# Four modulation chunks computed beside attention on VectorE instead of beside the deltanet on TensorE

## The chip, the cores and the metric

The kernel runs on one core of a Trainium2 chip. The metric is the device time of one execution in microseconds (us). The engines are TensorE (PE: matmuls, and PEld: its weight loads), VectorE (DVE), ScalarE (ACT), GpSimd (POOL) and SyncE (SP, which here issues nearly all DMA transfers). Each takes its instructions in the order in which the program holds them and waits at the first that isn't ready.

## What is computed

The reference is two blocks of a network over 512 tokens of width 1024. The first has a recurrence (hgrn2), a gated deltanet and a mixture of experts (MoE). The second has two layers: attention with a convolutional feed-forward part, then a gated unit with another. Each layer of the second block shifts, scales and gates its activations with a modulation vector, made from one conditioning vector:

```python
m_lat = (s_c @ ada_w[l] + ada_b[l])[:, None, :]          # 1024 -> 6 * 1024
sh1, sc1, g1, sh2, sc2, g2 = jnp.split(m_lat, N_MOD, axis=-1)
h_lat = modulate_2(rms_norm_2(x, mix_norm[l]), sh1, sc1)
...
x = x + g1 * y_lat
x = x + g2 * conv_ffn(modulate_2(rms_norm_2(x, ffn_norm[l]), sh2, sc2), ...)
```

The change is on this product for l = 0. The kernel cuts its 6144 columns into twelve chunks of 512, each with 2 MB of weights. Chunks 0 to 5 give sh1, sc1 and g1; chunks 6 to 9 give sh2 and sc2, which are first read by the normalisation ahead of the feed-forward part, behind attention; 10 and 11 give g2.

## The kernel before

All weights are float32 and come from memory once, each when it is used. A large product splits both sides into a high and a low part (whi and wlo from wraw or wrawx, hhi and hlo from the activations, lines 267 to 273) and adds three matmuls (lines 530 to 532). ScalarE makes the high parts and mostly VectorE the low ones.

The program is written as stages, and inside a stage as generators that are stepped in turn: in_turn (line 128) keeps up to `most` parts active, steps each once a turn, and steps `fill` once a turn too; what is left of fill when the parts are done runs behind them. Where an instruction stands on its engine is decided after that: the tile framework schedules the whole program with a simulated timeline, so work can be placed ahead of its place in the text where its data allow it. The order that results is fixed when the kernel is built.

There are two ways to make a modulation chunk:

- matvec_steps (line 334) on TensorE: two loads of 1 MB (wraw), eight matmuls of 512 columns whose stationary side is the conditioning vector (line 355), a copy on ScalarE (sq, line 359), four transposes (line 363), and two short sums on VectorE (mred, mod).
- matvec_on_dve (line 371) on VectorE: four loads of 512 KB (mvr), eight products of 128 x 512 with a per-partition scalar, added up in one tile (mva, lines 383 and 385), four transposes on TensorE (line 388), a reduction (mred, line 390) and a short sum into mod (line 391). The pool has one buffer of mva, and `bufs` of mvr.

```python
acc = pool.tile([P, 512], F32, name="mva")
...
nc.vector.tensor_scalar(acc, raw[:, k, :], c, None, op0=ALU.mult)
...
nc.vector.scalar_tensor_tensor(acc, raw[:, k, :], c, acc, op0=ALU.mult, op1=ALU.add)
```

The stages that the change touches, in order of time:

- The deltanet's core (dn_core, line 1199): twelve chunks of tokens, five active at a time, a new one every third turn. Its steps are small matmuls with copies and masked copies between them on ScalarE and VectorE. Its fill is matvec_steps with nine chunks of the modulation, one at two turns.
- The end of the MoE and the normalisation ahead of attention: TensorE makes the attention's projections of the context (hc in the tile hthi, pool hh) while moe_add adds the experts' result to x; then rstds_of_two (line 450) makes two inverse roots, one after the other, each with a step on GpSimd (rr, lines 456 to 463), TensorE spreads them, and norm_mod (lines 479 to 482) writes hhi and hlo for the projections of the latent tokens.
- The attention's core (attention_core, line 1676): eight heads in the order 0, 1, 4, 5, 6, 7, 2, 3, each with four units of 128 queries, three units active. A unit has scores (sc, line 1598), a maximum on VectorE (smax, line 1605), an exponential on ScalarE, transposes (line 1616; pT, line 1617) and the product with the values (av, lines 1742 and 1751). Heads 4 to 7 are differential: GpSimd adds two score tiles (line 1736), and VectorE normalises the result (qa, line 1789). The next head's operands are stacked in between (st, ks, kg, lines 1577 and 1588).
- The output projection (to_feature, line 637, and out_proj, line 554): TensorE transposes four blocks (line 650), which are split into hhi and hlo; the weights' splits whi and wlo are made beside them.

Of the kernel before, what the change touches and what calls it, by code (L numbers as in the profile page):

```python
# [127 lines left out]
def in_turn(parts, most, every, fill=None, newest=False):  # L128


    parts, active, turn, more = iter(parts), [], 0, True
    while active or more:
        if more and len(active) < most and turn % every == 0 or not active:
            part = next(parts, None)
            more = part is not None
            if more:
                active.append(part)
        turn += 1
        for part in list(active[::-1] if newest else active):
            if next(part, active) is active:  # L140
                active.remove(part)
        next(fill or iter(()), None)
    for _ in fill or ():
        pass
# [81 lines left out]
class Kern:  # L226
# [141 lines left out]
                                 bias[:, ch * 4:ch * 4 + 4].unsqueeze(2).to_broadcast([P, 4, 2]))  # L368
            yield

    def matvec_on_dve(self, pool, cc, w, bias, out, chunks, nk=2, bufs=3):

        nc = self.nc
        for ch in chunks:
            acc = pool.tile([P, 512], F32, name="mva")
            for k0 in range(0, KD, nk):
                raw = pool.tile([P, nk, 512], F32, name="mvr", bufs=bufs)
                nc.sync.dma_start(raw.rearrange("p k c -> p (k c)"), w.at(k0 // 4 * 4, 4, [(ch * 512, 512)])
                                  [:, k0 % 4 * 512:(k0 % 4 + nk) * 512])
                for k in range(nk):  # L380
                    c = cc[:, k0 + k, 0:1]
                    if k0 + k == 0:
                        nc.vector.tensor_scalar(acc, raw[:, k, :], c, None, op0=ALU.mult)
                    else:
                        nc.vector.scalar_tensor_tensor(acc, raw[:, k, :], c, acc, op0=ALU.mult, op1=ALU.add)  # L385
            p = self.ps.tile([P, 4, P], F32, name="aux", tag="aux")
            for s in range(4):
                nc.tensor.transpose(p[:, s, :], acc[:, s * P:s * P + P], self.ident)  # L388
            red = self.sp.tile([P, 4, 2], F32, name="mred")[:, :, 0]
            nc.vector.tensor_reduce(red, p, axis=AX.X, op=ALU.add)  # L390
            nc.vector.tensor_add(out[:, ch * 4:ch * 4 + 4, 0], red, bias[:, ch * 4:ch * 4 + 4])
            yield
# [1280 lines left out]
            wide(1024, [t["va"][:, a:b]])  # L1673
        return t

    def attention_core(self, t):

        nc = self.nc
        cp = self.pool("acore", 1)
# [73 lines left out]
            if qt == 3:  # L1753
                self.gqa_out(cp, t["qb"][:, :, i * P:i * P + P], av, sm)

        in_turn((unit(n, qt) for n in range(8) for qt in range(4)), 3, 1, None, True)

    def gqa_out(self, pool, o, av, sm):

# [155 lines left out]
def build(tc, aps):  # L1915
    nc = tc.nc
    with ExitStack() as ctx:
        K = Kern(ctx, tc, aps)
# [4 lines left out]
        cc = K.silu_cols("c", "c_ctx")  # L1923
        cc2 = K.silu_cols("c_2", "c_ctx_2")
        mod, mod0, mod1 = (K.cp.tile([P, 48, 2], F32, name=f"mod{n}") for n in range(3))
        ada0 = lambda f, chunks, *a: f(cc2, K.weights("ada_w_2"), K.vec("ada_b_2", 0, 48), mod0, chunks, *a)
        w, w_mod = K.weights("w_in"), K.weights("w_mod")
# [7 lines left out]
        with K.phase():  # L1935
            mp = K.pool("mix")
            oxh = mp.tile([P, 4, 512], F32, name="oxh")
            with ExitStack() as hstack:
                h = K.new_h(hstack.enter_context(tc.tile_pool(name="h", bufs=1, side="right")))
                with K.phase():  # L1940
                    hgp = K.pool("hgp")
                    hs0 = hgp.tile([P, 2, 4, P], F32, name="hs0")
                    t = {"v": hgp.tile([P, 4, 512], F32, name="hgv"), "kq": hgp.tile([P, 4, 3, T], F32, name="hgkq")}
                    with K.phase(4, 3):
                        hc = K.new_h(K.pool("hpc"), TC)
                        K.side = "right"
                        with K.phase():
                            xp = K.pool("xp")
                            with K.phase():
                                wm = K.matvec_steps(cc, w_mod, K.vec("b_mod"), mod, range(4), K.pool("mv"), 4)  # L1950
                                next(wm)
                                xc, accc = K.load_x(xp, aps["ctx"], TC, "xcT")
# [9 lines left out]
                        with K.phase():  # L1962
# [4 lines left out]
                            with tc.issue_after(K.loaded.ins):  # L1967
                                next(first)
                                x, acc = K.load_x(K.sp, aps["x"], T, t["kq"].rearrange("p h c t -> p (h c) t")[:, 0:KD, :])
# [38 lines left out]
                    xc, x, ab = K.dn_proj(st, h, w, oxd, dnd)  # L2008
                    K.split_on = [(None, None)]
            with K.phase(5, 0):  # L2010
                K.dn_core(op, xc, x, ab, ds0, oxd, ada0(K.matvec_steps, (0, 1, 2, 3, 4, 6, 7, 8, 9)))
            dstack.close()
            xp = ctx.enter_context(tc.tile_pool(name="xp", bufs=1, side="right"))
            x = K.reload(xp.tile([P, KD, T], F32, name="xT"), aps["x"])
# [23 lines left out]
        with K.phase():  # L2038
            K.wlp = K.pool("wl", 4)
            with K.phase(5, 0, 4):  # L2040
                K.moe(sd, reload_hc, ysd, hd, x, bs, mod, lambda pool: ada0(K.matvec_steps, range(5, 6), pool, 2, True))
            qp, st = right(qstack, "qst"), right(astack, "astore")
            with K.phase(4, 0, 1):
                hl = K.pool("hp")
                K.side = "right"
                with K.phase():
                    fn = K.vec("final_norm_w")
                    sums = K.pool("sums", space=PSUM).tile([P, 4, 2], F32, name="sums")
                    with K.phase():
                        K.moe_add(K.pool("ysp"), sums, ysd, x, mod[:, 40:48, :], fn)  # L2050
                    K.side = None
                    bx, bs = K.rstds_of_two(sums)
                    wn = K.sp.tile([P, KD], F32, name="wn")
                    nc.vector.tensor_mul(wn, mn, fn)
                    h = K.norm_mod(K.new_h(hl), x, bs, wn, mod0, 0, 1, 0)
                    K.scale_by(x, bx, fn)
                t = K.attention_proj(st, qp, (hc, h))
        with K.phase():
            K.attention_core(t)
        astack.close()  # L2060
        hstack.close()
        with K.phase(4):
            hp = K.pool("hp")
            with K.phase():
# [49 lines left out]
```

## Time and profile before

| | us |
|---|---|
| median of 3 runs (2381.67 to 2384.58) | 2383.46 |
| profiled execution: its own time | 2387.35 |
| profiled execution: span, first to last instruction | 2385.5 |
| TensorE matmuls busy | 2240.5 (94%) |
| VectorE busy | 1614.3 (68%) |
| ScalarE busy | 1200.8 (50%) |
| GpSimd busy | 620.3 (26%) |

Busy shares are averages over the span. A view by windows gives the same for a stretch; a timeline gives single instructions with their start, their duration and, in brackets, the idle time ahead of them with what ended it. Instructions of one kind that overlap are merged into one row (x8 is eight records). The granted clock is a share of TensorE's 2.4 GHz. All times are from the start of the span.

### The profile page before, as it was taken

The page shows a single profiled execution, that of the slowest core. Times are in us where ns is not written, and L with a number is a line of the kernel's source. Part 1 is how long each engine was busy: PE and PEld are TensorE (multiplying, and loading weights), DVE is VectorE, ACT ScalarE, POOL GpSimd, SP SyncE. Part 2 cuts the span into 40 slices and gives each one's busy share as a digit, 9 for nine tenths or more (in the row PEclk, how much of TensorE's full clock was granted, in tenths as well). Part 3 has the DMA queues.
Part 4 walks back from the last instruction along what each step waited for, and adds up shares of the span by engine and source line. Part 5 has one row for each costly group of instructions (what it writes and reads, how often), then busy time and mean ns, then how long its engine had stood idle before and what let it go on. Part 6 is the DMA issues. An engine that isn't in the chain of part 4 may idle for free.

```text
span 2385.5 us, 33834 instructions
## 1 busy us (share of the span) xinstructions
PE 2240.5 (94%) x13058; PEld 1880.5 (79%) x13058; DVE 1614.3 (68%) x2545; ACT 1200.8 (50%) x1969; POOL 620.3 (26%) x470
## 2 busy tenths in 40 slices
PE   6998989989988899999999999999999999999998
PEld 3988977758875677778778878878888988888887
DVE  4777877778855888886857865896673445553553
ACT  4455644456754677776337763432342433432433
POOL 2133544345421111100441422332333001110111
PEclk9999999999999899999999999999999999999999
DMA  8564004151045799997210002656433222323321
GB/s 317 186 222 143 28 1 153 46 219 74 2 177 230 281 395 368 372 379 267 77 39 1 2 36 107 237 193 231 148 131 102 102 89 71 106 73 113 106 74 60
DMA packets 68405, 355.24 MB, mean 149 GB/s; under 512 B 8065, under 2 KB 12817, under 8 KB 37009
## 3 DMA queue, kind: packets, MB, share of 16 engines
q1 hardware_dynamic: 62752, 333.94, 38.0%
q0 software_dynamic: 5488, 19.11, 3.3%
q8 instruction: 104, 1.70, 0.3%
q14 instruction: 61, 0.49, 0.1%
HBM read 334.45 MB, written 19.40 MB: 148 GB/s over the span
## 4 chain that ended last, share of the span: by engine, by line
PE 43%; DVE 5%; issue 1%; ACT 1%; DMA 0%; POOL 0%; SPq 0%; POOLq 0%; DVEq 0%; ACTq 0%
PE mm L531 12%; PE mm L532 12%; PE mm L530 12%; PE sc L1598 2%; PE av L1751 1%; PE aux L1616 1%; DVE mva L385 1%; PE av L1742 1%; DVE smax L1605 1%; DVE wlo L273 1%; PE aux L1587 0%; DVE cy L1868 0%; PE aux L388 0%; DVE st L1577 0%; DVE alo L273 0%
## 5 line engine op out<-in xcount | busy, mean ns | idle before, releaser
L530 PE MATMUL mm<-hhi,whi 128*128 128x512 f32 (+1 forms) x1184 | 438.0, 375 | 10.3 <-ACT whi L270 5.3
L531 PE MATMUL mm<-hlo,whi 128*128 128x512 f32 (+1 forms) x1184 | 441.5, 374 | 2.9 <-DVE hlo L482 2.9
L532 PE MATMUL mm<-hhi,wlo 128*128 128x512 f32 (+1 forms) x1184 | 438.7, 372 | 0.0
L270 ACT CAST whi<-wraw 128x1024 fp32r<-128x1024 f32 (+1 forms) x240 | 246.3, 1041 | 300.1 <-PE mm L531 223.5
L273 DVE TENSOR_TENSOR wlo<-wraw,whi 128x1024 fp32r<-128x1024 f32 (+1 forms) x203 | 249.3, 1244 | 179.9 <-ACT whi L270 179.1
L273 DVE TENSOR_TENSOR wlo<-wrawx,whi 128x1024 fp32r<-128x1024 f32 x190 | 229.0, 1230 | 94.3 <-ACT whi L270 93.0
L270 ACT CAST whi<-wrawx 128x1024 fp32r<-128x1024 f32 (+1 forms) x210 | 215.0, 1048 | 154.2 <-PE mm L531 106.1
L530 PEld LDWEIGHTS mm<-hhi,whi 128*128 128x128 f32 x1184 | 224.8, 191 | 49.4 <-ACT whi L270 5.9
L531 PEld LDWEIGHTS mm<-hlo,whi 128*128 128x128 f32 x1184 | 225.9, 191 | 41.5 <-DVE hlo L482 3.3
L532 PEld LDWEIGHTS mm<-hhi,wlo 128*128 128x128 f32 x1184 | 225.4, 191 | 38.0 <-issue 0.2
L530 PE MATMUL mm<-whi,hhi 128*128 128x512 f32 (+1 forms) x640 | 218.2, 346 | 6.3 <-ACT hhi L481 2.3
L532 PE MATMUL mm<-whi,hlo 128*128 128x512 f32 (+1 forms) x640 | 219.9, 347 | 3.8 <-DVE hlo L482 3.7
L531 PE MATMUL mm<-wlo,hhi 128*128 128x512 f32 (+1 forms) x640 | 219.6, 345 | 0.5 <-DVE wlo L273 0.4
L385 DVE SCALAR_TENSOR_TENSOR mva<-mvr,cc_c,mva 128x512 f32<-128x512 f32 x154 | 156.6, 1017 | 3.4 <-DMA mvr<-in_w_mod_dram 1.2
L1878 POOL TENSOR_TENSOR cy<-cy,csg 128x512 f32<-128x512 f32 x44 | 64.7, 1472 | 348.0 <-DVE cy L1870 332.5
L531 PE MATMUL mm<-alo,whi 128*128 128x512 f32 (+1 forms) x396 | 145.0, 366 | 0.0
L530 PE MATMUL mm<-ahi,whi 128*128 128x512 f32 (+1 forms) x396 | 144.7, 367 | 0.0
L532 PE MATMUL mm<-ahi,wlo 128*128 128x512 f32 (+1 forms) x396 | 144.4, 366 | 0.0
L273 POOL TENSOR_TENSOR wlo<-wraw,whi 128x1024 fp32r<-128x1024 f32 (+1 forms) x37 | 90.1, 2434 | 203.7 <-ACT whi L270 195.4
L530 PEld LDWEIGHTS mm<-whi,hhi 128*128 128x128 f32 x640 | 125.1, 196 | 20.3 <-ACT hhi L481 2.8
L532 PEld LDWEIGHTS mm<-whi,hlo 128*128 128x128 f32 x640 | 124.9, 196 | 19.7 <-DVE hlo L482 6.2
L531 PEld LDWEIGHTS mm<-wlo,hhi 128*128 128x128 f32 x640 | 125.0, 196 | 14.4 <-DVE wlo L273 1.3
(548 smaller groups left out, 4672.4 us busy)
## 6 DMA issues: line engine op xcount, KB each, us to landing
wrawx<-in_w_down_dram SPq DMA_DIRECT2D x32, 1024.0 KB, 9.1
wrawx<-in_w_gate_dram SPq DMA_DIRECT2D x30, 1024.0 KB, 9.0
wraw<-in_w_up_dram SPq DMA_DIRECT2D x30, 1024.0 KB, 9.2
wraw<-in_ffn_w_up_dram SPq DMA_DIRECT2D x30, 1024.0 KB, 4.8
mvr<-in_ada_w_dram SPq DMA_DIRECT2D x56, 512.0 KB, 4.5
wraw<-in_ada_w_dram SPq DMA_DIRECT2D x20, 1024.0 KB, 4.9
wraw<-in_w_in_dram SPq DMA_DIRECT2D x18, 1024.0 KB, 6.9
mvr<-in_w_mod_dram SPq DMA_DIRECT2D x32, 512.0 KB, 4.4
```

What stands on the lines that cost most here:

```text
L270: nc.scalar.copy(hi, src)
L273: (lo_eng or nc.vector).tensor_sub(lo, src, hi.bitcast(F32))
L385: nc.vector.scalar_tensor_tensor(acc, raw[:, k, :], c, acc, op0=ALU.mult, op1=ALU.add)
L530: nc.tensor.matmul(out, ahi, bhi, start=start, stop=False)
L531: nc.tensor.matmul(out, ahi, blo, start=False, stop=False)
L532: nc.tensor.matmul(out, alo, bhi, start=False, stop=stop)
L1598: nc.tensor.matmul(s[:, a:a + n], qs[:, qt * P:qt * P + P], ks[i][:, a:a + n], start=i == 0, stop=i == 1)
L1605: nc.vector.tensor_reduce(m, s[:, :768], axis=AX.X, op=ALU.max, negate=True)
L1616: nc.tensor.transpose(tp[:, j, :], p[:, (a + j) * P:(a + j + 1) * P], self.ident)
L1742: nc.tensor.matmul(av[:, qt, :], pt[:, k, :], hd["v"][:, k, :], start=k == 0, stop=k == 5)
L1751: nc.tensor.matmul(av[j * 64:j * 64 + 64, qt, :], hd["v"][:, k, :], pt[:, k, :], start=k == 0, stop=k == 5, tile_position=(0, j * 64))
L1878: nc.gpsimd.tensor_mul(y, y, sg)
```

## The change

Chunks 6 to 9 leave the fill of the deltanet's core, which keeps 0 to 4. The attention's core gets a fill: matvec_on_dve for these four, with three buffers of mvr and a new parameter, apart, that gives up five turns behind each load's two products. The pool for it is opened ahead of the attention's core, and the stack that holds hthi is closed before it, so that the loads' buffers and the accumulator can lie where hthi was.

```diff
-    def matvec_on_dve(self, pool, cc, w, bias, out, chunks, nk=2, bufs=3):
+    def matvec_on_dve(self, pool, cc, w, bias, out, chunks, nk=2, bufs=3, apart=0):
...
                         nc.vector.scalar_tensor_tensor(acc, raw[:, k, :], c, acc, op0=ALU.mult, op1=ALU.add)
+                for _ in range(apart):
+                    yield
...
-    def attention_core(self, t):
+    def attention_core(self, t, fill):
...
-        in_turn((unit(n, qt) for n in range(8) for qt in range(4)), 3, 1, None, True)
+        in_turn((unit(n, qt) for n in range(8) for qt in range(4)), 3, 1, fill, True)
...
-                K.dn_core(op, xc, x, ab, ds0, oxd, ada0(K.matvec_steps, (0, 1, 2, 3, 4, 6, 7, 8, 9)))
+                K.dn_core(op, xc, x, ab, ds0, oxd, ada0(K.matvec_steps, range(5)))
...
+        hstack.close()
         with K.phase():
-            K.attention_core(t)
+            mv = K.pool("mv")
+            K.attention_core(t, K.matvec_on_dve(mv, cc2, K.weights("ada_w_2"), K.vec("ada_b_2", 0, 48), mod0, range(6, 10), 2, 3, 5))
         astack.close()
-        hstack.close()
```

In the changed program most lines carry a number that is higher by one to three, so line 385 is 386 there. Three places of the order show where the scheduler put the work. The first is VectorE between the MoE and the attention; before:

```order
L536 SCALAR_TENSOR_TENSOR xT<-aux,mod_79,xT 128x512 x4
L273 TENSOR_TENSOR wlo<-wraw,whi 128x1024
L456 TENSOR_SCALAR rr_11553<-sums 128x8
L457 TENSOR_SCALAR rr_11553<-rr_11553 128x4
L459 TENSOR_TENSOR rr_11553<-rr_11553 128x4
L460 TENSOR_TENSOR rr_11553<-rr_11553 128x4
L461 TENSOR_SCALAR rr_11553<-rr_11553 128x4
L463 TENSOR_TENSOR rr_11553<-rr_11553 128x4
L479 SCALAR_TENSOR_TENSOR nmt<-xT,nma,aux 128x256 x4
```

and with the change:

```order
L273 TENSOR_TENSOR wlo<-wraw,whi 128x1024
L384 TENSOR_SCALAR mva<-mvr,cc_c_75 128x512
L386 SCALAR_TENSOR_TENSOR mva<-mvr,cc_c_75,mva 128x512 x2
L459 TENSOR_SCALAR rr_11461<-sums 128x8
L386 SCALAR_TENSOR_TENSOR mva<-mvr,cc_c_75,mva 128x512
L460 TENSOR_SCALAR rr_11461<-rr_11461 128x4
L386 SCALAR_TENSOR_TENSOR mva<-mvr,cc_c_75,mva 128x512 x2
L462 TENSOR_TENSOR rr_11461<-rr_11461 128x4
...
L466 TENSOR_TENSOR rr_11461<-rr_11461 128x4
L386 SCALAR_TENSOR_TENSOR mva<-mvr,cc_c_75,mva 128x512
L482 SCALAR_TENSOR_TENSOR nmt<-xT,nma,aux 128x256 x4
L386 SCALAR_TENSOR_TENSOR mva<-mvr,cc_c_75,mva 128x512
```

All eight products of chunk 6 now stand among the two inverse roots. On SyncE, three of its loads stand behind the weight load ahead of them, then one more weight load, then the fourth.

The second is VectorE at the end of the attention's core; qb is the last head's output, the splits under it belong to the output projection; before:

```order
L1617 COPY pT<-aux 128x384 x3
L1768 TENSOR_TENSOR qb<-qb,av 128x4x128
L273 TENSOR_TENSOR wlo<-wraw,whi 128x1024
L273 TENSOR_TENSOR hlo_14802<-aux,hhi_14801 128x512
L273 TENSOR_TENSOR wlo<-wraw,whi 128x1024
L273 TENSOR_TENSOR hlo_14802<-aux,hhi_14801 128x512 x3
L273 TENSOR_TENSOR wlo<-wrawx,whi 128x1024 x2
```

and with the change:

```order
L1620 COPY pT<-aux 128x384 x4
L393 TENSOR_REDUCE mred<-aux 128x4
L384 TENSOR_SCALAR mva<-mvr,cc_c_75 128x512
L1771 TENSOR_TENSOR qb<-qb,av 128x4x128
L394 TENSOR_TENSOR mod_80<-mred,vec 128x4
L386 SCALAR_TENSOR_TENSOR mva<-mvr,cc_c_75,mva 128x512 x7
L393 TENSOR_REDUCE mred<-aux 128x4
L394 TENSOR_TENSOR mod_80<-mred,vec 128x4
L475 SCALAR_TENSOR_TENSOR nma<-mod_80,vec 128x8
L273 TENSOR_TENSOR wlo<-wraw,whi 128x1024 x2
L273 TENSOR_TENSOR wlo<-wrawx,whi 128x1024 x2
L273 TENSOR_TENSOR hlo_14814<-aux,hhi_14813 128x512 x4
```

Seven products and the reduction of chunk 9 stand between qb and the splits, and all four wlo now come ahead of the first hlo. On SyncE, eight loads of mvr (the eighth to fifteenth) stand behind the attention's small loads, then the wrawx load of the output projection, then the sixteenth load of mvr.

The third is TensorE at the same place; before:

```order
L1751 MATMUL av<-pT,kv 64x128 x6
L650 MATMUL aux<-cst,qa 128x128 x4
L1751 MATMUL av<-pT,kv 64x128 x5
L650 MATMUL aux<-cst,qa 128x128 x8
L530 MATMUL mm<-hhi_14801,whi 128x512 x2
L650 MATMUL aux<-cst,qa 128x128 x4
L531 MATMUL mm<-hlo_14802,whi 128x512
```

and with the change:

```order
L1754 MATMUL av<-pT,kv 64x128 x6
L391 MATMUL aux<-cst,mva 128x128 x4
L1754 MATMUL av<-pT,kv 64x128 x5
L391 MATMUL aux<-cst,mva 128x128 x4
L653 MATMUL aux<-cst,qa 128x128 x12
L533 MATMUL mm<-hhi_14813,whi 128x512 x4
L653 MATMUL aux<-cst,qa 128x128 x4
L534 MATMUL mm<-hlo_14814,whi 128x512
```

The transposes of chunk 8 stand where four of the projection's stood, and those of chunk 9 ahead of all twelve. Chunk 7's eight products stand on VectorE behind the second differential head's sums (odr), one at a time between the maxima and splits of the next heads; those of chunk 8 stand likewise in the last two heads. In the feed-forward stage behind, the same fourteen chunks are made as before, with a few products in other places.

## Rows read from the trace of the kernel before

**Rows 1.** The page, part 1: busy us, share of the span, instructions.

```profile
PE 2240.5 (94%) x13058; PEld 1880.5 (79%) x13058; DVE 1614.3 (68%) x2545; ACT 1200.8 (50%) x1969; POOL 620.3 (26%) x470
```

**Rows 2.** Windows, deltanet's core: us, busy (x instructions) by engine, clock, DMA.

```profile
514.52:562.57 48.05, 44.69 (x482) 35.46 (x480) 36.00 (x63) 31.89 (x64) 19.73 (x18) 1.00 0.51 196
562.57:606.47 43.90, 40.76 (x446) 37.20 (x444) 39.64 (x78) 30.70 (x64) 24.87 (x21) 1.00 0.00 1
```

**Rows 3.** Timeline of TensorE, one chunk in the core: start, us, instruction.

```profile
521.62 1.92 PE L355 MATMUL aux<-wraw,cc_c 128*32 128x512 f32 x16
...
523.48 0.40 PE L1018 MATMUL mm<-dnxi,dny 128*128 128x128 f16 x4
...
527.86 0.61 PE L363 MATMUL aux<-cst,sq 128*128 128x128 f32 x4
...
528.30 0.39 PE L1018 MATMUL mm<-dnxi,dny 128*128 128x128 f16 x4
```

**Rows 4.** Timeline of TensorE: the last matmul that reads the context's activations.

```profile
1131.13 0.40 PE L532 MATMUL mm<-whi,hthi 128*128 128x512 f32 x1
```

**Rows 5.** Tile mvr: ns min/median/max of the products, and the loads' landing.

```profile
L385 DVE SCALAR_TENSOR_TENSOR mva<-mvr,cc_c,mva x154: 734/748/2986, 77.5 to 1772.7; 128x512 f32<-128x512 f32 x154
...
L383 DVE TENSOR_SCALAR mva<-mvr,cc_c x22: 475/479/2491, 77.0 to 1760.7; 128x512 f32<-128x512 f32 x22
...
DMA to landing us min/median/max: 3.2/4.5/7.7
```

**Rows 6.** Timeline of VectorE, chain of the inverse roots.

```profile
1133.13 1.23 DVE L273 TENSOR_TENSOR wlo<-wraw,whi 128x1024 fp32r<-128x1024 f32 x1 [1.50 <-ACT whi L270]
...
1135.72 0.17 DVE L456 TENSOR_SCALAR rr<-sums 128x8 f32<-128x8 f32 x1 [1.37 <-PE sums L1510]
...
1137.25 0.16 DVE L459 TENSOR_TENSOR rr<-rr 128x4 f32<-128x4 f32 x1 [1.16 <-POOL rr L431]
...
1140.42 1.66 DVE L479 SCALAR_TENSOR_TENSOR nmt<-xT,nma,aux 128x256 f32<-128x256 f32 x4 [1.33 <-PE aux L438]
```

**Rows 7.** Windows, attention's core: differential heads, then the last two heads.

```profile
1345.00:1360.00 15.00, 12.56 (x94) 11.30 (x93) 14.98 (x32) 11.86 (x26) 5.42 (x6) 1.00 0.00 1
...
1405.00:1424.00 19.00, 19.00 (x205) 15.14 (x201) 8.64 (x15) 8.94 (x21) 0.00 (x0) 1.00 0.00 1
```

**Rows 8.** Line 390, the reduction of one chunk: ns min/median/max.

```profile
L390 DVE TENSOR_REDUCE mred<-aux x22: 679/688/693, 93.4 to 1782.3; 128x4 f32<-128x512 f32 x22
```

**Rows 9.** Timeline of VectorE: the four qa products of two heads.

```profile
1347.21 2.96 DVE L1789 SCALAR_TENSOR_TENSOR qa<-od,odss,subln 128x128 f32<-128x128 f32 x4
...
1370.65 1.13 DVE L1789 SCALAR_TENSOR_TENSOR qa<-od,odss,subln 128x128 f32<-128x128 f32 x4
```

**Rows 10.** Timeline of GpSimd beside the first of these.

```profile
1347.40 1.86 POOL L1736 TENSOR_TENSOR pexp<-pexp 128x768 f32<-128x768 f32 x1 [1.96 <-ACT pexp L1735]
```

**Rows 11.** Timeline of TensorE behind the last head.

```profile
1423.71 0.87 PE L1751 MATMUL av<-pT,kv 128*64 128x128 f32 x10
...
1428.11 0.48 PE L531 MATMUL mm<-hlo,whi 128*128 128x512 f32 x1
```

**Rows 12.** Timeline of VectorE behind the last head.

```profile
1424.69 0.69 DVE L1768 TENSOR_TENSOR qb<-qb,av 128x512 f32<-128x512 f32 x1 [2.79 <-PE av L1751]
1425.82 1.22 DVE L273 TENSOR_TENSOR wlo<-wraw,whi 128x1024 fp32r<-128x1024 f32 x1 [0.44 <-ACT whi L270]
1426.96 0.68 DVE L273 TENSOR_TENSOR hlo<-aux,hhi 128x512 fp32r<-128x512 f32 x1
```

**Rows 13.** Timeline of SyncE's queue at the same place.

```profile
1424.72 0.33 SPq L506 DMA_DIRECT2D wrawx<-in_attn_w_out_dram  x1
```

**Rows 14.** Windows, behind an idle TensorE: PEclk stands after POOL's time.

```profile
681.00:690.00 9.00, 3.24 (x25) 2.92 (x25) 4.98 (x8) 5.82 (x19) 4.40 (x3) 0.91 0.45 141
690.00:695.00 5.00, 5.00 (x14) 3.87 (x15) 5.00 (x14) 4.18 (x11) 1.02 (x1) 0.50 1.00 382
```

## The prediction

> **What bounds the kernel now.** I read the share of busy time first: TensorE is busy 94% of the span, VectorE 68% [rows 1]. That is an average over unlike stages, so next come the stretches in which the change takes away and adds work, each with its busy times, and then the order of single instructions in them.
>
> Four stretches matter. In the deltanet's core, from 514.5 to 562.6 us, TensorE is busy 44.69 of 48.05 us and VectorE 36.00; in the 43.90 us behind it, where no modulation chunk is left, TensorE has 40.76 and VectorE 39.64 [rows 2]. Each stretch holds three starts of a chunk of tokens. Both engines bound this core. Between the MoE and the attention, VectorE runs a short serial chain (two inverse roots) on which TensorE waits [rows 6]. In the differential heads VectorE is the bound: 14.98 of 15 us, TensorE 12.56 [rows 7]. In the last two heads it is TensorE, 19.00 of 19, and VectorE has 8.64 [rows 7]. Behind the last head VectorE's splits (wlo, hlo) release the first matmuls of the output projection [rows 11, 12].
>
> **What is taken away: the deltanet's core.** Four of nine chunks leave. TensorE's 16 records of one chunk fill it from 521.62 to 523.48, 1.86 us, and its four transposes from 527.86 to 528.30, 0.44 us [rows 3]: 2.30 us a chunk, 9.2 us for four, all inside 514.5 to 562.6. What that is worth has two bounds. If TensorE alone sets the pace, 44.69 - 9.2 = 35.5 us of work at the later stretch's busy share (40.76 / 43.90 = 0.93) take 38.2 us: 9.9 us gained. If these three rounds of the core cannot get shorter than the three behind them (43.90 us), 4.2 us. VectorE lies between: 36.00 us at its share there (39.64 / 43.90 = 0.90) take 39.9 us, 8.1 us gained. I take **-8**, since VectorE is the next bound; the ends are -9.9 and -4.2. The four copies on ScalarE (busy 31.89 of the 48.05 us) and the eight short sums on VectorE that go too, and the eight loads, are counted at nothing: the work beside them goes on as before.
>
> **What is added, in four places.** A chunk is four loads of 512 KB, a first product of 0.48 us and seven of 0.75 us on VectorE [rows 5], four transposes (0.44 us, as above) and a reduction of 0.69 us [rows 8]: 5.7 us of products, 6.4 us in all. The short sum into mod is left out of the count.
>
> *Chunk 6, in the chain of inverse roots.* The order puts three products ahead of the first step (rr from sums), one behind it, two in the first wait for GpSimd, one ahead of the first normalisation (nmt) and one behind it. The buffers lie where the context's activations lay, and the last matmul that reads those begins at 1131.13 and takes 0.40 [rows 4]; so the first load goes out at 1131.5 and lands 3.2 us later at the soonest, 4.5 at the median [rows 5]: 1134.7 to 1136.0. VectorE is free at 1134.4, and rr began at 1135.72 [rows 6]. Three products (0.48 + 2 x 0.75) put it at 1136.7 to 1138.0: 1.0 to 2.3 late. The product behind it adds 0.75; the two inside the wait (1.5 us in about 1.2) add 0.3; the one ahead of nmt needs the fourth load, which reuses the first buffer and goes out behind a weight load, so it lands some 4.5 us after 1136.5, at 1141, when nmt (1140.42 before) has already slid to 1142.5; the last adds 0.75. Sum 2.8 to 4.1; TensorE waits for this chain. I take **+3**; the ends are +1.5 (the products fill idle time of VectorE) and +5 (the fourth load lands after 7.7 us, the maximum of its row).
>
> *Chunk 7, in the differential heads.* Its 6.4 us fall on the stretch in which VectorE is full [rows 7]; about 1 us of idle just ahead takes up some. Then there is GpSimd: the four qa products took 2.96 us where a GpSimd sum of 1.86 us ran beside them, and 1.13 us the second time [rows 9, 10], so an operation of VectorE that meets one waits 1.8 us. I take **+5.5**; the ends are +2 (TensorE has 2.4 us of idle in which to catch up, and later heads have slack) and +8 (two such meetings).
>
> By the Trainium skill, page SBUF — State Buffer, section Who interferes with whom, a VectorE instruction with two inputs in SBUF and a GpSimd one that reads SBUF exclude each other for a whole instruction. These rows agree: 2.96 less 1.13 is the length of the sum beside it. Taken for each of the two or three sums that stand there, the rule would make this term about 9 and the total 17.
>
> *Chunk 8, in the last heads.* TensorE is full, VectorE half idle: the products hide. The transposes of chunks 6 to 8 do not (3 x 0.44). **+1**, ends 0 and +2.5.
>
> *Chunk 9, behind the last head.* This is the largest term. A chunk has one accumulator, and chunk 8's transposes stand five matmuls before the last av on TensorE; chunk 9's first product waits for them. So seven of its products stand on VectorE behind the last qb product, ahead of all splits for the output projection; and on TensorE its transposes stand ahead of all the projection's transposes and matmuls. The time: qb ends at 1425.4 [rows 12]; products two to six, 5 x 0.75, end at 1429.1. The last two need the sixteenth load, whose buffer is free only after the second product (1426.2) and which stands in SyncE's queue behind the 1 MB wrawx load of 1424.72 [rows 13]: with 4.5 us it lands at 1430.7, and the products end at 1432.2. Transposes 0.44, reduction 0.69: 1433.3. Then four wlo, 1.14 us apart (1425.82 to 1426.96, [rows 12]), and the first hlo, 0.6: 1438.5. The first matmul on hlo began at 1428.11 [rows 11]; it slides by 10.4, less 0.5 since two more L530 matmuls now stand ahead of it. TensorE is nearly idle meanwhile; after it had been busy only 3.24 of 9 us elsewhere, the granted clock was 0.50, the 1.2 GHz level, for 5 us [rows 14], in which half of 5 us of work is lost. I take **+12**; the ends are +7.5 (the sixteenth load is there in time, no clock loss) and +15 (it lands after 7.7 us, and the clock falls).
>
> **Sum.** -8 + 3 + 5.5 + 1 + 12 = +13.5 us. The profiled execution took 2387.35, so 2400.9; it stands 3.9 above the median of the runs, 2383.46, so **2397.0** as such a median.
>
> **Rivals.**
> 1. *Faster.* TensorE is at 94% and VectorE at 68%: four chunks leave the full engine and hide on the other. For it: chunk 8's place. Against it: the order at the end, where VectorE is not idle cover but the only way to the projection. If all products hid, -8 and 4 x 0.44 of transposes give -6.2: 2377. It decides at the last av: chunk 9 would have to be reduced by 1428.1, and its first product cannot begin before 1424. Chance 0.07. The Trainium skill, page Perfetto Trace Analysis, section Identifying the Most-Contended Engine, says to optimise the engine of highest occupancy first; going by that alone this would be the outcome, and the rows of this case speak against it.
> 2. *No change to be told.* The core gains all 9.9, the sixteenth load is in time (+7.5), chunks 6 and 7 cost their low ends (3.5): +1 to +4.5, 2385 to 2388. For it: the low ends share one cause, loads that land early. Chance 0.15.
> 3. *Much slower.* The core's rounds keep the later length (-4.2), GpSimd meets the products twice, the sixteenth load is held by wrawx: 5 + 8 + 2.5 + 15 - 4.2 = +26, 2410. Above +20 it has a chance of 0.13.
>
> **The numbers.** A forecast of +5 to +20 keeps 0.65. A measurement of this kernel tells 0.2%, 4.8 us, from no change. Slower by more: 0.65 + 0.13 = 0.78; within: 0.15; faster: 0.07. The range runs from 2386 (+2.5: rival 2's upper part is in) to 2407 (+23.5); the ends of all terms together, +1 and +26, are less likely than 2 in 10.
>
> **What would show it.** Right: the core's stretch with five chunks shortened by 7 to 9 us; eight products among the inverse roots, nmt 2 to 4 us later against the end of the context's matmuls; between the last av and the first hlo matmul some 14 us instead of 3.5, with TensorE waiting on mva and the clock near 0.50 behind it; products on the chain in the differential heads. Wrong: a gap behind the last av under 8 us (then the sum is near zero), a core shortened by less than 4 or more than 10, or a change of several us in the feed-forward stages, whose products only change places and which I count at nothing.

## The result and the profile after

The changed kernel takes 2406.93 us (median of four runs), the kernel before beside it 2382.57: a ratio of 1.0105, 95% interval 1.0087 to 1.0122. It is slower by 21 to 29 us. The forecast was 2397.0; 2406.9 lies at the upper end of the range, and the ratio times the median of 2383.46 gives 2408.5, just above it. The profiled execution took 2406.73, with a span of 2404.9: 19.4 more than the one shown of before, where 13.5 were forecast.

The page of the changed kernel, part 1, answers to [rows 1]: VectorE has 20.8 us more work, and TensorE, from which four chunks were taken, is no less busy.

```profile
PE 2240.0 (93%) x12994; PEld 1882.9 (78%) x12994; DVE 1635.1 (68%) x2577; ACT 1202.4 (50%) x1965; POOL 621.2 (26%) x470
```

The windows of the deltanet's core, columns as in [rows 2]: the same three rounds, then the three behind them.

```profile
512.83:553.27 40.44, 36.04 (x402) 32.16 (x400) 32.14 (x56) 29.58 (x60) 21.09 (x18) 1.00 0.07 26
553.27:597.17 43.90, 40.81 (x445) 37.15 (x443) 38.27 (x77) 30.97 (x64) 25.16 (x21) 1.00 0.01 1
```

48.05 us became 40.44: 7.6 gained. Then VectorE's timeline among the inverse roots; it answers to [rows 6].

```profile
1127.70 0.49 DVE L384 TENSOR_SCALAR mva<-mvr,cc_c 128x512 f32<-128x512 f32 x1 [1.37 <-DMA mvr<-in_ada_w_dram]
1128.22 1.54 DVE L386 SCALAR_TENSOR_TENSOR mva<-mvr,cc_c,mva 128x512 f32<-128x512 f32 x2
1129.68 0.16 DVE L459 TENSOR_SCALAR rr<-sums 128x8 f32<-128x8 f32 x1
...
1134.54 0.75 DVE L386 SCALAR_TENSOR_TENSOR mva<-mvr,cc_c,mva 128x512 f32<-128x512 f32 x1 [0.42 <-DMA mvr<-in_ada_w_dram]
1135.45 1.66 DVE L482 SCALAR_TENSOR_TENSOR nmt<-xT,nma,aux 128x256 f32<-128x256 f32 x4 [0.16 <-PE aux L441]
```

VectorE waits 1.37 us for the first load and 0.42 for the last, and seven of the eight products stand ahead of nmt. Last, the timelines of four engines behind the last head, put together in order of time; [rows 11 to 13] show the place before.

```profile
1425.85 0.87 PE L1754 MATMUL av<-pT,kv 128*64 128x128 f32 x10
1426.87 0.33 SPq L509 DMA_DIRECT2D wrawx<-in_attn_w_out_dram  x1
1426.96 0.68 DVE L1771 TENSOR_TENSOR qb<-qb,av 128x512 f32<-128x512 f32 x1
1427.57 6.28 POOL L273 TENSOR_TENSOR hlo<-qb,hhi 128x512 fp32r<-128x512 f32 x4 [31.68 <-ACT hhi L270]
1427.62 9.13 DVE L386 SCALAR_TENSOR_TENSOR mva<-mvr,cc_c,mva 128x512 f32<-128x512 f32 x7
1429.42 0.33 SPq L379 DMA_DIRECT2D mvr<-in_ada_w_dram  x1
1436.90 1.09 PE L391 MATMUL aux<-cst,mva 128*128 128x128 f32 x4 [10.19 <-DVE mva L386]
1437.78 2.77 PE L653 MATMUL aux<-cst,qa 128*128 128x128 f32 x12
1439.11 2.36 DVE L273 TENSOR_TENSOR wlo<-wraw,whi 128x1024 fp32r<-128x1024 f32 x2
1441.39 2.35 DVE L273 TENSOR_TENSOR wlo<-wrawx,whi 128x1024 fp32r<-128x1024 f32 x2
1443.66 1.88 DVE L273 TENSOR_TENSOR hlo<-aux,hhi 128x512 fp32r<-128x512 f32 x3
1445.12 0.77 PE L534 MATMUL mm<-hlo,whi 128*128 128x512 f32 x1
```

TensorE waits 10.19 us for the products. Its first hlo matmul begins 17.0 us later than before, and the last row of av only 2.1 us later. Behind the wait its granted clock is at the 1.2 GHz level (window, columns as in [rows 14]); and ScalarE, whose casts whi stand ahead of every wlo, had by the profile waited for chunk 9's transposes too (its timeline; before, whi waited 1.56 us for av):

```profile
1436.90:1440.00 3.10, 3.10 (x15) 3.10 (x16) 1.90 (x4) 1.97 (x3) 0.00 (x0) 0.50 0.00 0
1438.03 2.00 ACT L270 CAST whi<-wraw 128x1024 fp32r<-128x1024 f32 x2 [8.97 <-PE aux L391]
```

The seven products take 9.13 us, where seven of 0.75 are 5.3. Taken one by one (the view of line 386 in 1427.6 to 1433; min/median/max in ns), the first four are twice as long as elsewhere, each beside one of GpSimd's four splits:

```profile
L386 DVE SCALAR_TENSOR_TENSOR mva<-mvr,cc_c,mva x4: 1631/1633/1767, 1427.6 to 1432.8; 128x512 f32<-128x512 f32 x4
```

One more stage changed, and the prediction had counted it at nothing: the first feed-forward. These are the groups by line of its products, before and after, from the last residual of the attention's projection to the first residual of the down projection (150.8 us before, 157.1 after):

```profile
L385 DVE SCALAR_TENSOR_TENSOR mva<-mvr,cc_c,mva 128x512 f32<-128x512 f32 x56 | 60.0, 1071 | 0.6
```

```profile
L386 DVE SCALAR_TENSOR_TENSOR mva<-mvr,cc_c,mva 128x512 f32<-128x512 f32 x61 | 59.6, 977 | 0.8
L384 DVE TENSOR_SCALAR mva<-mvr,cc_c 128x512 f32<-128x512 f32 x9 | 7.3, 810 | 4.6 <-DMA mvr<-in_ada_w_dram 4.6
```

The scheduler now puts five more products and a ninth chunk's first one ahead of that residual. TensorE has 25 matmuls more there too (713 against 688), so the length of this stretch says little. From the same start to the seventh residual of the down projection both kernels hold the same 884 matmuls and 213 instructions of VectorE. Here are the windows of that stretch, before and after, each with TensorE's wait for the products (us in total, times, longest):

```profile
1474.03:1669.10 195.07, 188.50 (x884) 156.96 (x883) 160.78 (x213) 70.30 (x96) 62.30 (x30) 0.98 0.60 208
PE aux L388 <- DVE mva L385: 4.7, 4, 1.6
```

```profile
1491.29:1689.07 197.78, 189.12 (x884) 157.03 (x883) 161.68 (x213) 71.17 (x96) 61.13 (x30) 0.98 0.60 205
PE aux L391 <- DVE mva L386: 6.9, 6, 2.3
```

TensorE is busy 97% of it before and VectorE 82%. With the change it is 2.7 us longer, and 2.2 of that is time in which TensorE, about to transpose a chunk's sum, waits for the chunk's last product.

The table cuts each profiled execution at the same five places: the first and the last matmul on identb in the deltanet's core, the first nmt behind the MoE, the last av matmul, the fifth residual behind the attention. Each entry is a difference of two starts from the views by line, the last one runs to the end of the span, and each row is a single execution.

| us | to core | core | to nmt | to last av | to residual | to the end |
|---|---|---|---|---|---|---|
| before | 508.3 | 166.7 | 465.4 | 283.9 | 34.2 | 927.0 |
| after | 506.6 | 159.1 | 469.8 | 290.9 | 49.3 | 929.2 |
| e1 chunk 9 in core | 506.4 | 161.0 | 469.4 | 291.2 | 35.4 | 923.8 |
| e2 left out | 508.0 | 159.0 | 467.2 | 282.5 | 34.2 | 931.1 |
| e3 held | 506.6 | 159.1 | 467.2 | 290.0 | 48.4 | 922.1 |
| e4 GpSimd's queue | 505.5 | 159.0 | 471.6 | 290.3 | 49.3 | 931.0 |
| e5 paced | 505.0 | 159.0 | 466.4 | 288.9 | 34.2 | 926.0 |
| e6 paced, other order | 506.6 | 159.1 | 466.7 | 289.8 | 34.1 | 930.8 |
| e7 MoE | 505.5 | 159.0 | 492.8 | 282.0 | 34.2 | 931.1 |
| e8 two in projection | 507.2 | 159.0 | 467.9 | 285.1 | 36.0 | 922.4 |
| e9 three in projection | 510.4 | 159.0 | 467.4 | 282.8 | 36.1 | 932.2 |
| e10 hlo on VectorE | 506.4 | 159.0 | 470.4 | 290.3 | 46.9 | 931.1 |

The first column, where no edit reaches (e2's memset alone stands there), runs from 505.0 to 510.4: so much differs between executions by itself. Shorter columns repeat better: the core is 159.0 or 159.1 us in the ten kernels with five chunks in it, and the third column 466.4 to 467.9 in the six changed ones without products or chunks there. The last column falls into two groups, by the order in the first feed-forward: after, e2, e4, e6, e7 and e10 have the one with the ninth chunk early (929 to 931), before, e1, e3, e5 and e8 the other (922 to 927); e9, at 932.2, is told below. The groups part within that feed-forward: from the fifth residual to the seventh of the down projection the first group takes 213.3 to 214.7 us, the second 207.3 to 210.6.

### The profile page after: what moved, and what is told of

Its sections match the earlier page's. It is cut to its first block, busy times and chain, and to the rows that moved or that the text cites. A ratio compares the mean times of both kernels' runs of the same rounds, so it can differ in the third digit from the quotient of the medians.

```text
span 2404.9 us, 33759 instructions
## 1 busy us (share of the span) xinstructions
PE 2240.0 (93%) x12994; PEld 1882.9 (78%) x12994; DVE 1635.1 (68%) x2577; ACT 1202.4 (50%) x1965; POOL 621.2 (26%) x470
## 4 chain that ended last, share of the span: by engine, by line
PE 39%; DVE 7%; issue 2%; ACT 1%; POOL 1%; DMA 0%; SPq 0%; POOLq 0%; DVEq 0%; ACTq 0%
PE mm L534 11%; PE mm L535 11%; PE mm L533 11%; DVE mva L386 3%; PE sc L1601 1%; PE av L1754 1%; PE aux L1619 1%; DVE wlo L273 1%; DVE smax L1608 1%; DVE cy L1871 1%; DVE cy L1873 0%; PE av L1745 0%; POOL cy L1881 0%; PE aux L1590 0%; DVE nmt L482 0%
## 5 line engine op out<-in xcount | busy, mean ns | idle before, releaser
L386 DVE SCALAR_TENSOR_TENSOR mva<-mvr,cc_c,mva 128x512 f32<-128x512 f32 x182 | 179.9, 988 | 4.5 <-DMA mvr<-in_w_mod_dram 1.5
L534 PEld LDWEIGHTS mm<-wlo,hhi 128*128 128x128 f32 x640 | 125.0, 196 | 15.1 <-DVE wlo L273 2.0
```

The costliest lines, as they stand in the source:

```text
L534: nc.tensor.matmul(out, ahi, blo, start=False, stop=False)
```

## The experiments

**e1: chunk 9 back into the core.**

```diff
-                K.dn_core(op, xc, x, ab, ds0, oxd, ada0(K.matvec_steps, range(5)))
+                K.dn_core(op, xc, x, ab, ds0, oxd, ada0(K.matvec_steps, (0, 1, 2, 3, 4, 9)))
...
-            K.attention_core(t, K.matvec_on_dve(..., range(6, 10), 2, 3, 5))
+            K.attention_core(t, K.matvec_on_dve(..., range(6, 9), 2, 3, 5))
```

> Chunk 9 alone goes back into the deltanet's core, on TensorE; chunks 6 to 8 stay as products between the attention's units. Theory (the stretch behind the last head costs about 16 us, and one chunk costs the core about 2): the first hlo matmul of the output projection begins about 4 us behind the last av matmul, as before the change, and the time is 2406.9 - 16 + 2 = 2393. Rival (the wait behind the last head only takes the place of a wait for the output projection's weights, so most of it stays): less than 6 us come back, 2401 or more.

Measured: 2391.12, ratio to before 1.0033 (1.0020 to 1.0045). The stretch behind the last av falls from 49.3 to 35.4, the core pays 1.9 for one chunk. The theory holds; of the 15.8 us by which it beats the changed kernel, a part is the feed-forward's order, which went back too.

**e2: chunks 6 to 9 left out.** Their columns are zeros here, so the output is another.

```diff
-            K.attention_core(t, K.matvec_on_dve(...))
+            nc.gpsimd.memset(mod0[:, 24:40, 0], 0.0)
+            K.attention_core(t, None)
```

> Chunks 6 to 9 are left out altogether (their 16 columns of the second layer's modulation are set to zero by GpSimd ahead of the attention). So the core is short and nothing is added in the attention. Theory (chunk 6 costs 3.9 us among the inverse roots, 6.3 in the attention's units, chunk 9 about 16 behind them): 2406.9 - 26 = 2381, about 2 to 7 us under the kernel before. Rival (what the core gives back is lost again in the MoE's waits or the feed-forward, whoever does the chunks): 2385 or more, no better than before.

Measured: 2381.78, ratio 0.9990 (0.9977 to 1.0002). The number of the theory came out, but the gain on the kernel before, 2 to 7 us in the theory, is not clear of the noise. The table says why it is small: the core keeps its 7.7, nothing is lost in the attention, and 4.1 is lost behind, in the feed-forward, where no chunk was left out. That is the rival's mechanism; the order there is the changed kernel's.

**e3: the products held behind the attention's start.**

```diff
+        self.mark = nc.vector.tensor_reduce(m, s[:, :768], axis=AX.X, op=ALU.max, negate=True).ins
...
+                with self.tc.issue_after(self.mark) if apart else ExitStack():
                     for k in range(nk):
...
-            K.attention_core(t, K.matvec_on_dve(...))
+            K.attention_core(t, chain([None], K.matvec_on_dve(...)))
```

The last line starts the fill with one empty turn.

> Every product of chunks 6 to 9 is held, on VectorE, behind the last row maximum of the attention's scores that stands ahead of it in the program; so none can stand among the two inverse roots, and chunk 6 falls into the first two heads, where VectorE was busy 9.5 of 15 us. The rest is the same. Theory (the products among the inverse roots cost 3.9 us; in the first heads VectorE has room): nmt comes back to its place behind the context, 2403. Rival (chunk 6 costs there what it cost ahead, since TensorE and VectorE alternate in the heads): 2407.

Measured: 2393.87, ratio 1.0044 (1.0031 to 1.0057), 13 us better than the changed kernel where 4 were expected. The stretch up to nmt gives back 2.6, as much as with the chunk left out, and the heads' column does not grow though chunk 6 is now in it. The other 7 us stand in the last column. Of these, 4.0 lie ahead of the seventh residual of the down projection: the feed-forward's order turned back, by the hold or by the empty turn, which e3 does not tell apart. The other 3.1 lie behind it, at a granted clock of 1.00 against 0.99, and no edit explains them.

**e4: loads on GpSimd's queue.**

```diff
-                nc.sync.dma_start(raw.rearrange("p k c -> p (k c)"), ...)
+                (nc.gpsimd if apart else nc.sync).dma_start(raw.rearrange("p k c -> p (k c)"), ...)
```

> The 16 loads of chunks 6 to 9 are issued by GpSimd instead of SyncE. Theory (the last two products of chunk 9 wait because the sixteenth load stood in SyncE's queue behind wrawx and a wait of its own; seven products of 0.75 us took 9.13 us, 3.9 more than their sum): the load goes out with the second product's end, the products end up to 3.9 us sooner, 2403. Rival (the 4 us that a load takes set the end, whichever queue issues it, or GpSimd's own sums are held up by the issues): 2407 or more.

Measured: 2408.56, ratio 1.0104 (1.0077 to 1.0132), no gain, as the rival has it. The timeline shows why this run could not tell whether the load was what the products waited for:

```profile
1427.51 4.61 POOL L273 TENSOR_TENSOR hlo<-qb,hhi 128x512 fp32r<-128x512 f32 x3 [12.04 <-ACT hhi L270]
1427.56 7.70 DVE L386 SCALAR_TENSOR_TENSOR mva<-mvr,cc_c,mva 128x512 f32<-128x512 f32 x5
1432.07 0.56 POOL L379 DMA_DIRECT2D mvr<-in_ada_w_dram  x1
1436.17 1.54 DVE L386 SCALAR_TENSOR_TENSOR mva<-mvr,cc_c,mva 128x512 f32<-128x512 f32 x2 [0.90 <-DMA mvr<-in_ada_w_dram]
```

The sixteenth load now stands behind three of GpSimd's splits and is 2.7 us later than on SyncE. And five products take 7.70 us with their loads there: they are long by themselves, beside the splits. e10 tests that.

**e10: the four splits on VectorE.**

```diff
-            self.split(hi, lo, p, None, self.nc.gpsimd if b in done else None)
+            self.split(hi, lo, p)
```

> The changed kernel, with one thing else: the four splits hlo<-qb behind the last head are done by VectorE, between chunk 9's products, and no longer by GpSimd beside them. Theory (four of chunk 9's seven products took 1.77, 1.63, 1.63 and 1.63 us beside these four GpSimd splits, where 0.75 is their length alone; the sixteenth load was not what they waited for): every product 0.75 us, the products and the four splits together 7.8 us in place of 9.13, the first hlo matmul 1.4 us sooner, 2405.5. Rival (the load sets the end, the products' length is the wait for it): the last two products still begin 7 us behind the first, 2407 or more.

Measured: 2403.97, ratio 1.0075 (1.0056 to 1.0093).

```profile
1427.25 0.74 DVE L386 SCALAR_TENSOR_TENSOR mva<-mvr,cc_c,mva 128x512 f32<-128x512 f32 x1
1427.91 1.89 DVE L273 TENSOR_TENSOR hlo<-qb,hhi 128x512 fp32r<-128x512 f32 x3
1429.72 0.74 DVE L386 SCALAR_TENSOR_TENSOR mva<-mvr,cc_c,mva 128x512 f32<-128x512 f32 x1
1430.38 0.68 DVE L273 TENSOR_TENSOR hlo<-qb,hhi 128x512 fp32r<-128x512 f32 x1
1430.98 3.90 DVE L386 SCALAR_TENSOR_TENSOR mva<-mvr,cc_c,mva 128x512 f32<-128x512 f32 x5
```

Products and splits together take 7.6 us in place of 9.13, no load is waited for, and the stretch is 2.4 us shorter. The interval overlaps the changed kernel's, so it is the trace that bears the theory out. VectorE does both jobs sooner alone than the two engines do side by side: in the changed kernel it was GpSimd's splits, not the load behind wrawx, that made the products late.

**e5 and e6: paced, and the feed-forward's order.** On top of e3's hold:

```diff
+            K.attention_core(t, chain([None], mv6, [None] * 2, mv7, [None] * 20, mv8_9))
```

where each mv is matvec_on_dve for the chunks named, with apart=1, and each None is an empty turn. e6 has 19 for 20.

> Four chunks stay in the attention, but all products are held behind the scores' row maximum that stands ahead of them in the program, and the fill is paced: a chunk in five turns, chunks 6 and 7 in the first two heads, then twenty turns of nothing, chunks 8 and 9 behind the differential heads, all reduced before the last av matmul. The first feed-forward has the order of instructions that it has in the kernel before. Theory (the core keeps its 8 us; no price among the inverse roots or behind the last head; 1.8 us of transposes on TensorE and some 2 us where products meet a full VectorE): 2383.1 - 8 + 4 = 2379, below the kernel before. Rival (VectorE's products delay the units wherever they stand, about half of 4 x 6.4 us): 2387, above it.

> As e5_paced, with nineteen empty turns in place of twenty. The attention is nearly the same; but the program's order in the first feed-forward comes out as it does in the kernel of the change (a SyncE load of mvr, ScalarE casts and GpSimd splits in other places). Theory (that order alone costs about 4 us between the attention's output projection and the first down projection's end): 4 us above e5_paced. Rival (the 4 us there come from when loads land, not from the order): within 1 us of e5_paced.

Measured: e5 2381.44, ratio 0.9994 (0.9980 to 1.0007); e6 2389.81, ratio 1.0029 (1.0012 to 1.0045). e5 lies between its theory and its rival. With nothing left behind the last head that stretch is 34.2 as before, but the attention pays 5 us for the four chunks: from the second head's output to the last differential head's it takes 90.9 us, before 76.6, and 9.3 are given back ahead of that and behind it. e6's theory holds: the order alone costs. The medians of the two differ by 8.4 us, the profiled executions by 7.6: 4.8 in the last column, 0.9 in the attention, 1.6 ahead of the core, where nothing was edited. The groups by line of the first up projection, e5 and then e6, are those of before and of the changed kernel:

```profile
L387 DVE SCALAR_TENSOR_TENSOR mva<-mvr,cc_c,mva 128x512 f32<-128x512 f32 x56 | 60.0, 1072 | 0.6
```

```profile
L387 DVE SCALAR_TENSOR_TENSOR mva<-mvr,cc_c,mva 128x512 f32<-128x512 f32 x61 | 59.6, 977 | 0.8
```

and so are the windows of the stretch with the same matmuls, to the seventh residual of the down projection:

```profile
1469.06:1663.02 193.96, 187.41 (x884) 155.82 (x883) 160.80 (x213) 70.31 (x96) 62.35 (x30) 0.99 0.61 209
```

```profile
1471.89:1670.66 198.77, 190.35 (x884) 158.23 (x883) 162.04 (x213) 71.05 (x96) 60.86 (x30) 0.97 0.59 204
```

All 4.8 us lie here. TensorE waits for products 6.7 us in place of 4.7, and the same matmuls take it 2.9 us more, at a granted clock of 0.97 against 0.99.

**e7: the chunks in the MoE, on TensorE.** The fill there gets range(5, 10) in place of range(5, 6), the attention None.

> Chunks 6 to 9 go neither into the core nor into the attention: they follow chunk 5 in the MoE, as TensorE matmuls among the routing's steps, where TensorE was busy 37 of 60 us (740 to 800). The attention is free of them; the feed-forward has the order of the changed kernel. Theory (TensorE has room there, 4 x 2.3 us hide; the core keeps 8): 2381.8 as with the chunks left out, plus at most 1. Rival (their eight loads of 1 MB stand in SyncE's queue ahead of the experts' weights, some 6 us a chunk at 330 GB/s): 2390 to 2405.

Measured: 2408.11, ratio 1.0114 (1.0094 to 1.0134). The stretch up to nmt is 25.6 us longer than in e2, without the chunks. The rival holds, and the time is above its range; the view of line 355 (the chunks' matmuls) and SyncE's timeline:

```profile
L355 PE MATMUL mm<-wraw,cc_c x80: 592/1060/1063, 747.9 to 784.8; 128*32 128x512 f32 x80
...
  DMA wraw<-in_ada_w_dram: 16.6, 9
...
760.19 18.92 SPq L344 DMA_DIRECT2D wraw<-in_ada_w_dram  x6
```

TensorE waits 16.6 us for loads, and most of its matmuls there last 1060 ns where the shortest took 592, at a granted clock of 0.64 from 748 to 785 us.

**e8 and e9: the products behind the attention.** As e5, but with two empty turns at the start of the fill (e8) or three (e9), and with chunks 8 and 9 (e8), or 7 to 9 and only chunk 6 in the heads (e9), between the residuals of the output projection, two steps of the fill behind each group of matmuls from its second quarter on, held behind the last residual or split:

```diff
                             self.mm3(p[cb][:, ts], ...)
+                        for _ in range(steps if oc else 0):
+                            next(fill, None)
```

> Chunks 6 and 7 as in e5_paced, in the first two heads; chunks 8 and 9 go behind the attention, into the second quarter and on of its output projection, each product held behind the last residual or split that stands ahead of it, where TensorE is full and VectorE was busy 14 of 40 us (1430 to 1470 in e5_paced). The first feed-forward keeps the order that it has in the kernel before. Theory (products cost where VectorE is on the units' path, and nothing where only TensorE is full): the differential heads take 77 us again in place of 91, with 1.8 us of transposes to pay: 3 to 4 us under e5_paced, 2378, and under the kernel before by more than an interval. Rival (the loads and splits of the projection's and the feed-forward's weights are delayed by the products): no better than e5_paced.

> As e8_two_in_projection, with only chunk 6 in the first two heads and chunks 7, 8 and 9 in the output projection; the third ends among the last residuals, just ahead of the normalisation that reads it. Theory (the first heads pay more than the projection): 1 us under e8. Rival (chunk 9's reduction is late for the normalisation, which costs 2 us or more): above e8.

Measured: e8 2379.39, ratio 0.9976 (0.9963 to 0.9990); e9 2385.24, ratio 1.0000 (0.9989 to 1.0010). e8 beats both kernels, the one before by 0.1 to 0.4%; its theory holds there, while the intervals of e5 and e8 overlap. Its windows of the projection (columns as in [rows 2]):

```profile
1423.00:1432.00 9.00, 8.96 (x40) 6.78 (x38) 7.95 (x9) 4.60 (x9) 6.54 (x4) 1.00 0.99 390
1432.00:1462.00 30.00, 30.00 (x159) 25.79 (x158) 25.57 (x31) 10.00 (x13) 10.54 (x6) 1.00 0.60 221
```

TensorE stays full while VectorE goes to 25.57 of 30 us. Of the 7.7 us that the core gives, the attention takes 1.2, the projection 1.8. In e9 the rival holds: the third chunk's last load is late, and the last residual stands behind it in VectorE's order:

```profile
1468.72 3.48 DVE L389 SCALAR_TENSOR_TENSOR mva<-mvr,cc_c,mva 128x512 f32<-128x512 f32 x2 [2.16 <-DMA mvr<-in_ada_w_dram]
1472.12 0.48 DVE L542 SCALAR_TENSOR_TENSOR xT<-mm,mod,xT 128x256 f32<-128x256 f32 x1
1473.48 0.69 DVE L396 TENSOR_REDUCE mred<-aux 128x4 f32<-128x512 f32 x1 [0.88 <-PE aux L394]
```

The normalisation waits for both: from the fifth residual to the first convolution of the feed-forward it takes 43.6 us (from 1455.7 to 1499.3), and 35.0 in e8 (from 1455.2 to 1490.2). That is most of its loss in the last column; the feed-forward behind has the order of before. The profiled execution is the slowest of e9's twelve, 4.4 us above their median, so the wait may be shorter in others.

## Why the prediction was wrong in its size

**The core: the size right, the reason not.** Forecast -8, measured -7.6 in the three rounds and in the whole column; one chunk is worth 1.9 (e1). The rounds became shorter than those behind them, so the end at -4.2 was no limit. But the 8 was chosen because VectorE was to be the next bound, with its 36.00 us of work at a share of 0.90. It has 32.14 us in the 40.44, a share of 0.79, and TensorE 36.04, a share of 0.89. The chunks' short sums, counted at nothing, are 2.4 of the 3.9 us that VectorE lost (in the groups by line 2.8 us before and 0.4 after). That the figure of 39.9 came near 40.44 is luck.

**Chunk 6 among the inverse roots: right.** Forecast +3. The column up to nmt grew by 4.4, but 1.8 of it are there without the products too (e2, e3), so the chunk costs 2.6. The mechanism was there: against the end of the context's matmuls nmt comes 3.1 us later, and TensorE's wait for the inverse roots grew from 3.56 to 6.26 us. Where the 1.8 us come from, in the MoE, stays open; no run was made on it.

**Chunks 7 and 8 in the heads: right.** Forecast 6.5; that column grew by 7.0, which includes the last product behind the first nmt. e2 shows that without chunks it is 1.4 shorter than before, so the price may be up to 8.4, inside the forecast's ends (2 to 10.5). One of chunk 7's seven products met a GpSimd sum and took 2.11 us, 1.4 more than alone, where 1.8 were priced.

**Chunk 9 behind the last head: the right mechanism, mis-sized.** Forecast +12, ends 7.5 and 15; measured 15.1 from the last av to the fifth residual, of which e1 shows 13.9 to be chunk 9's. The step that failed is the sum from qb to the first hlo matmul, and in it the term "products two to six, 5 x 0.75". From the end of qb the whole sum was forecast at 13.1 us (1425.4 to 1438.5) and took 17.5 (1427.64 to 1445.12).

Of these 4.4 us, 2.3 are the products, which ended 9.1 us behind qb and not 6.8. Four of them took 1.63 to 1.77 us: 3.7 us more than their length alone. The sixteenth load, which the forecast had as what delays the last two, went out at 1429.42, when the first of the row's seven had ended. The trace has the landing of four of the sixteen loads, 3.7 to 4.9 us behind their issue; by these it was there by 1434.3, and the sixth of the row, which is the first to need it, began at 1435.2. e10 took the splits away from GpSimd, and the products ran at 0.74 to 0.78 each with no wait. An estimate from these numbers: with no split on either engine, the load of e10, out at 1428.02, would have landed 3.7 to 4.9 us later, and with two products of 0.75 behind it they end 6.0 to 7.2 us behind the first one's start (1427.25), so the meeting with GpSimd is worth 2 to 3 us. Of the rest of the 4.4, 0.8 are the transposes at half clock (the reduction began 1.28 us behind the products, not 0.44), 0.4 two short sums that were left out, and 0.8 the last four transposes, which stand between the first hlo and its matmul (0.5 before). Behind the first hlo matmul the forecast added 2.0 us more, 2.5 for the clock less 0.5; measured are 0.2. The clock fell as forecast, but part of its price lay ahead of that matmul.

The prediction priced meetings with GpSimd in the differential heads [rows 9, 10] and forgot that GpSimd splits qb behind the last head too. The rule it cited from the Trainium skill, page SBUF — State Buffer, section Who interferes with whom (a VectorE instruction with two SBUF inputs and a GpSimd one that reads SBUF exclude each other), was needed here as much as at chunk 7; the products' 1.63 us beside splits, and 0.74 without, agree with it. The trace does not show it for every GpSimd instruction: two products of chunk 6 took 0.75 us each while GpSimd's 128x4 step of the inverse root ran, from 1130.71 to 1132.24.

The prediction also has VectorE's order alone as what holds back wlo. By the profile ScalarE's whi waited for chunk 9's transposes as well, in e10 too, so the first wlo could not begin before 1439.1, when it did, even with VectorE free. whi does not read those transposes. That its buffer lies where the accumulator was is likely, but not shown, and no run moved either.

**The feed-forward: the step that was left out.** The prediction counted "the feed-forward stages, whose products only change places" at nothing, and named several us there as a sign that it is wrong. They cost 2.2 us in the changed kernel's last column (2.7 up to the seventh residual of the down projection), and 4.8 between e5 and e6, whose only edit is one empty turn in the attention. With the new order TensorE waits longer for the products ahead of a chunk's transposes: 6.9 us in place of 4.7, and 6.7 in place of 4.7 between e5 and e6.

**The base.** -1.7 (ahead of the core) - 7.6 + 4.4 + 7.0 + 15.1 + 2.2 = 19.4, where 13.5 were forecast: 5.9 of the miss. The other 4.0 are the step from the profiled execution to the median. The prediction took off 3.9, the height of before's profiled execution over its median; the changed kernel's profiled execution lies at its median (2406.73 and 2406.93). Against the kernel before run beside it, the medians differ by 24.4 us, 4.9 more than the profiled executions do, and no column can say where these stand.

**The rivals.** Much slower, above +20, is what the runs show by ratio, but not by its path: the core's rounds did not keep their length and wrawx did not hold the load. Its GpSimd meetings were there, one at chunk 7 and four behind the last head.

## What to carry to other kernels

VectorE products were cheap here only where TensorE alone set the pace: against the kernel without them (e2) the same four chunks cost 26 us among inverse roots, differential heads and behind the last head (2.6, 8.4, 15.1), and 5.1 in the first heads and the output projection (e8: 0.7 up to nmt, 2.6 in the attention, 1.8 in the projection). At each place where products go, list what GpSimd does at that moment and price every meeting, not only those in the stretch one has in mind. Where a scheduler writes the order, compare the orders of all later stages too, and look for places where the fullest engine waits for what has moved; a single empty turn moved 4.8 us here. Before a term is taken from the engine that is "next bound", count what the change takes from that engine as well.

## What the hardware showed that was not expected

A VectorE product of two SBUF inputs and a GpSimd split of two ran in step: four products at 1.63 to 1.77 us beside four splits that took 6.28 together, 0.74 without. One engine doing both in turn (7.6 us for seven products and four splits) beat two engines side by side (9.13 for the products alone).

The profile of one execution can be 4 us off its kernel's median with no edit (the first column of the table spans 5.4 us), so a sum of terms of this size is carried to the median only to within that.
